# Dealing TensorE's filling work in steps of three products in a hybrid attention, SSD and gating layer

## The chip, the core and the metric

The kernel runs on one core of a Trainium2 chip. The metric is the device time of one execution in microseconds (us); lower is better. The engines are TensorE (PE in the profile, its weight loads PEld), VectorE (DVE), ScalarE (ACT), GpSimd (POOL) and SyncE (SP, which issues nearly all DMAs, strictly in the order of its row).

## What is computed

One layer for 640 tokens, 128 of a prompt and 512 of a latent grid, 2048 channels, float32. A large input projection feeds three branches; each branch's result (1024 channels) is multiplied by its own weights w_br (1024 x 2048), gated, added up and projected once more:

```python
def _layer(x, cvec, p, ctx):
    ...
    h = (_rms(x, p['g_pre']) * (1 + scale) + shift).astype(x.dtype)
    proj = jnp.matmul(h, p['w_in'])
    q, k, v, g_a, xbc, z, dt_raw, u, v_c, g_c, g_m = jnp.split(proj, _in_splits(), -1)
    ...
    o_a = o_a * jax.nn.silu(g_a)
    o_b, h_f, h_b = _ssm_branch(xbc, z, dt_raw, p, h0_f, h0_b)
    o_c = _sgu_branch(u, v_c, g_c, p)
    gate_a, gate_b, gate_c = jnp.split(jax.nn.sigmoid(g_m), 3, -1)
    merged = (gate_a * jnp.matmul(o_a, p['w_br_a']) + gate_b * jnp.matmul(o_b, p['w_br_b'])
              + gate_c * jnp.matmul(o_c, p['w_br_c']))
    y = _rms(jnp.matmul(merged, p['w_out']), p['g_post'])
    return (x + gate * y).astype(x.dtype), (k, v, h_f, h_b)
```

Branch a is attention with 16 heads (a prompt part, and a window of the grid plus 128 context keys), branch b a bidirectional state-space scan (SSD) with 16 heads and a norm over its 1024 channels, branch c a gating unit (SGU). The outputs are the layer's result, the new keys and values of the prompt and the new states of the scan.

## The kernel before

**Products.** A float32 value x is kept as two tiles, x_hi (rounded to fp32r, a ScalarE copy) and x_lo (x - x_hi, a VectorE subtraction); a product is then three fp32r products: hi by hi, hi by lo, lo by hi. Weights come in as raw tiles (wraw) and are split the same way into whi and wlo (L135 and L136). The 640 tokens are two halves of 320 columns.

**Stages.** After the projections, branch c is ready in SBUF as eight operands of 128 channels (oh, ol). The SSD (b) and the attention (a) still have to be computed. They are many small matmuls with VectorE, ScalarE and GpSimd work between, so the kernel mixes them with the long products of w_br. Those are 48 blocks: branch c, then b, then a, with 16 blocks d of 128 output channels each. A block has 8 operands k x 2 halves x 3 products = 48 products. `br_halves` (L824) is a generator that yields after each half, 24 products into one PSUM bank (tile bk); VectorE then multiplies the bank by the gate of that block (tile gt, a ring of two) and GpSimd adds it to the merged tile. `fill(n)` (L852) takes n halves from it. In the trace all these products, and those of the SSD and the attention, have the line of a helper (L807); the tile bk names the filling work, sm the rest.

**SSD** (L858 to L950). For each of the 8 pairs of heads t, `states(t)` loads tokens (xtok), lets GpSimd weight them (xw, L882), multiplies them with btok into two PSUM tiles, from which VectorE chains the states hst (L899) and ScalarE copies the new state out (so, L904); `outputs(t)` reads hst, A, E and xtok into two more PSUM tiles, VectorE makes y2, GpSimd gates it with zs, and it goes to memory as o_b. The loop runs the states one pair ahead: states(0), states(1), fill(2), outputs(0), fill(2), states(2), fill(2), outputs(1) and so on, 29 halves in all. This work's pool (ssd2) is left at its end, and the attention's pool (att) takes its place.

**Attention** (L952 to L1141). For each pair of heads j there are 5 units: b = None (prompt) and 0 to 3. A unit is `scores` (q by k, and by the context keys kc), a softmax by VectorE and ScalarE (tiles mx, s, rc; lines L990 to L997), `turned` (transposes of the probabilities, copied out as pt by ScalarE, L1081), and `values` (pt by vk and cv). Scores run one unit ahead. The list pace gives each of the 40 units a half or none, 33 in all. Pair 0's q, k, v and bias and all of kc and cv are loaded at the beginning of the attention (`loads`, L1014, and L1115, L1116), later pairs one pair ahead; the values are transposed by token (vk, L1038) by `by_tok`.

**From branch to branch.** When branch c's last block is done, branch b's operands must stand in the very slots of c's operands. `b_operands` (L958) loads the eight tiles of o_b through a staging ring of three (ost), scales each on VectorE and splits it (oh by ScalarE, L588, ol by VectorE, L589); it is called in unit 2. Its norm is a row factor that is made by `b_norm` and `b_row` and multiplied in later. Branch a's operands (oa, then oah and oal) are loaded after the last unit (L1146); two more halves of b, the rest of it, stand behind that, then a's 16 blocks, two halves each.

**Order.** The order of the matmuls is that of the text: each `step()` ties its first matmul behind the last one issued. All else is placed by a scheduler by dependences, so that a load may stand far ahead of its place in the text if its tile is free, and each engine then runs its own row in order. An engine that waits holds all that stands behind it.

## Time and profile before

| | before |
|---|---|
| runs | 2575.22, 2579.98, 2577.57 us |
| median | 2577.57 us |
| the profiled execution's own time | 2580.66 us |
| its span in the trace | 2578.9 us |
| granted TensorE clock, mean of the span | 0.987 |
| busy: PE, PEld | 95%, 89% |
| busy: DVE, ACT, POOL | 66%, 42%, 31% |
| DMA | 413.76 MB, mean 160 GB/s |

The span is what the rows of the trace cover; the device time is 1.8 us longer. A busy share is an average over the whole program. The granted clock is the share of TensorE's full speed that the chip gave it in a stretch: 1.00 is 2.4 GHz, 0.50 is 1.2 GHz. The parts that the change touches lie between 1797 and 2338 us: the SSD with c's blocks to 1955, the attention with the rest of c's blocks and nearly all of b's to 2208, then a's blocks.

### The profile page before, as it was taken

To read this page: it belongs to the slowest core of one execution; us is meant where nothing else is said; L and a number is where in the kernel's file an instruction comes from. 1 tells how busy PE (TensorE), PEld (TensorE's weight loads), DVE (VectorE), ACT (ScalarE), POOL (GpSimd) and SP (SyncE) were. 2 spreads that over 40 slices of the span, in tenths; PEclk is the share of its full clock that TensorE was granted. 3 is DMA by queue.
4 is the path that set the end of the run, shared out by engine and by line. 5 is a ranking of instruction groups with operands and counts; after the bars stand their busy time and mean duration, and the time that the engine had idled before them with its cause. 6 is when DMAs were issued, how large, how long until landed. Compare 5 with 4: busy or idle time off the path is not lost. (4 is left out here: it accounts for less than half of the span.)

```text
span 2578.9 us, 43223 instructions
## 1 busy us (share of the span) xinstructions
PE 2447.0 (95%) x16615; PEld 2306.5 (89%) x16615; DVE 1713.0 (66%) x2776; ACT 1085.4 (42%) x2343; POOL 805.5 (31%) x372
## 2 busy tenths in 40 slices
PE   6999989999999999999999999999897999999998
PEld 4579979999999999999999999989896888898886
DVE  4344678888887887777777767776334555437974
ACT  4122333444444455565555455555114555322222
POOL 2100035444444443333333434342231232331002
PEclk9999999999999999999999999999998999999999
DMA  9943533333333434534343443436777444445545
GB/s 375 340 163 106 175 119 121 103 115 114 108 108 118 142 131 145 166 132 152 126 170 122 131 155 130 143 126 210 280 254 253 165 156 124 134 125 188 190 135 167
DMA packets 152169, 413.76 MB, mean 160 GB/s; under 512 B 16981, under 2 KB 28538, under 8 KB 150938
## 3 DMA queue, kind: packets, MB, share of 16 engines
q1 hardware_dynamic: 149658, 409.95, 47.5%
q8 instruction: 130, 2.13, 0.3%
q10 hardware_dynamic: 2304, 1.05, 0.1%
q14 instruction: 77, 0.63, 0.1%
HBM read 336.12 MB, written 74.81 MB: 159 GB/s over the span
## 5 line engine op out<-in xcount | busy, mean ns | idle before, releaser
L167 DVE TENSOR_TENSOR wlo<-wraw,whi 128x512 fp32r<-128x512 f32 x448 | 613.4, 1386 | 121.8 <-ACT whi L166 113.5
L166 ACT CAST whi<-wraw 128x512 fp32r<-128x512 f32 x448 | 274.8, 616 | 313.0 <-PE acca L235 148.3
L135 ACT CAST whi<-wraw 128x512 fp32r<-128x512 f32 (+1 forms) x238 | 140.2, 592 | 412.4 <-PE bk L807 127.2
L236 PE MATMUL acca<-hh,wlo 128*128 128x320 f32 x896 | 280.8, 313 | 22.8 <-DVE wlo L167 22.7
L166 ACT CAST whi<-s 128x512 fp32r<-128x512 f32 x336 | 202.2, 617 | 199.6 <-PE sm L235 77.7
L234 PE MATMUL acca<-hh,whi 128*128 128x320 f32 x896 | 278.6, 311 | 3.9 <-ACT whi L166 3.9
L167 DVE TENSOR_TENSOR wlo<-s,whi 128x512 fp32r<-128x512 f32 x336 | 232.6, 692 | 74.6 <-ACT whi L166 70.3
L235 PE MATMUL acca<-hl,whi 128*128 128x320 f32 x896 | 277.3, 310 | 0.0
L190 POOL TENSOR_TENSOR s<-wraw 128x1024 f32<-128x1024 f32 x56 | 145.4, 2597 | 367.5 <-DMA wraw<-in_w_nt 235.7
L136 DVE TENSOR_TENSOR wlo<-wraw,whi 128x512 fp32r<-128x512 f32 (+1 forms) x218 | 147.7, 680 | 141.4 <-ACT whi L135 138.2
L191 POOL TENSOR_TENSOR s<-s,wraw 128x1024 f32<-128x1024 f32 x56 | 151.1, 2698 | 263.8 <-DVE wlo L167 263.7
L198 POOL TENSOR_TENSOR s<-wraw,s 128x1024 f32<-128x1024 f32 x56 | 138.6, 2475 | 219.0 <-issue 193.8
L236 PEld LDWEIGHTS acca<-hh,wlo 128*128 128x128 f32 x896 | 168.7, 188 | 30.4 <-DVE wlo L167 30.4
L234 PEld LDWEIGHTS acca<-hh,whi 128*128 128x128 f32 x896 | 168.8, 188 | 5.2 <-ACT whi L166 5.2
L235 PEld LDWEIGHTS acca<-hl,whi 128*128 128x128 f32 x896 | 168.8, 188 | 0.0
L807 PE MATMUL bk<-oh,whi 128*128 128x320 f32 x512 | 164.1, 321 | 0.7 <-DVE c L250 0.7
L807 PE MATMUL bk<-ol,whi 128*128 128x320 f32 x512 | 159.4, 311 | 0.0
L807 PE MATMUL bk<-oh,wlo 128*128 128x320 f32 x512 | 159.3, 311 | 0.0
L192 POOL TENSOR_TENSOR wraw<-wraw 128x1024 f32<-128x1024 f32 x56 | 152.1, 2716 | 4.3
L236 PE MATMUL sm<-t4h,wlo 128*128 128x320 f32 x448 | 141.2, 315 | 12.9 <-DVE wlo L167 12.8
L236 PE MATMUL sm<-hh,wlo 128*128 128x320 f32 x448 | 138.5, 309 | 2.8 <-DVE wlo L167 2.8
L236 PE MATMUL sm<-t12h,wlo 128*128 128x320 f32 x448 | 138.7, 310 | 1.2 <-DVE wlo L167 1.2
(390 smaller groups left out, 6978.1 us busy)
## 6 DMA issues: line engine op xcount, KB each, us to landing
wraw<-in_w_nt SPq DMA_DIRECT2D x240, 512.0 KB, 3.7
wm<-in_w_ms SPq DMA_DIRECT2D x64, 512.0 KB, 7.4
wraw<-in_w_br SPq DMA_DIRECT2D x48, 512.0 KB, 4.3
wm<-in_w_mg SPq DMA_DIRECT2D x32, 512.0 KB, 3.9
wraw<-in_w_out SPq DMA_DIRECT2D x31, 512.0 KB, 3.9
g_gate<-sg SPq DMA_DIRECT2D x48, 320.0 KB, 2.4
gt<-g_gate SPq DMA_DIRECT2D x48, 320.0 KB, 3.5
bias<-in_bias SPq DMA_DIRECT2D x8, 1152.0 KB, 7.8
```

The costliest lines, as they stand in the source:

```text
L135: S.copy(hi[:, :n], rv)
L136: eng.tensor_tensor(lo[:, :n], rv, hi[:, :n].bitcast(F32), op=ALU.subtract)
L166: S.copy(hi, src[:, i:i + 512])
L167: V.tensor_sub(lo, src[:, i:i + 512], hi.bitcast(F32))
L190: G.tensor_tensor(s1, a21, a22, op=ALU.add)
L191: G.tensor_tensor(s2, s1, a11, op=ALU.subtract)
L192: G.tensor_tensor(a21, a11, a21, op=ALU.subtract)
L198: G.tensor_tensor(s2, a12, s2, op=ALU.subtract)
L234: TE.matmul(ps, wh, bh, start=(k == 0 and i not in (2, 3)), stop=False, skip_group_check=True)
L235: TE.matmul(ps, wh, bl, start=False, stop=False, skip_group_check=True)
L236: mm = TE.matmul(ps, wl, bh, start=False, stop=(k == n - 1), skip_group_check=True)
L807: newest[0] = TE.matmul(*args, **kw)
```

## The change

The unit of filling becomes a step: the three products of one operand and one half (`br_steps` in place of `br_halves`), and all counts are given in steps, eight to a half.

- **SSD.** `weighted` (xtok and xw) is cut off from `states`. The order is now fill(16), then for each pair states(t), weighted(t+1), fill(8), outputs(t), fill(24); after outputs(6) it is fill(8), after outputs(7) none. That is 232 steps, as many products as the 29 halves.
- **First attention tiles.** In pair 6's place of the text `first_loads(0)` loads kc for pair 0 alone (64 KB; kc now comes by pairs) and the first of three rows of the bias (b0) into the outer pool, and q, k, v of pair 0 into two free slots and one tile of ost. The other two rows of the bias are loaded with `loads`.
- **Attention.** fill(8) stands before the first scores; the pace is 8, 8 and then 6 or 7 steps in each of the other 38 units, 248 steps. The 24 steps that are left of branch b stand behind the last unit, fill(24).
- **Passage by the contraction.** In blocks 0 and 15 of each branch the operand k is the outer loop and the half the inner one, with a PSUM bank for each half, so that operand k is read in two neighbouring steps. In all other blocks the halves come one after the other, as before.
- **b's operands** are asked for in unit 1; ScalarE scales while it rounds (one activation) and VectorE subtracts with the scaling in one instruction, so eight VectorE multiplications are dropped. The staging ring ost has two tiles instead of three. b_norm and b_row are each called a unit or two earlier.
- **Buffers.** Gates (gt) 2 to 3; xtok 2 to 3; xT, btok, xw 2 to 1; the operands oa of branch a pass through a ring of four instead of eight tiles. The four columns of a softmax stand in one tile.

```diff
     def gate_ring(name):
-        return p2.tile([P, T], F32, tag="gt", name=name, bufs=2)
+        return p2.tile([P, T], F32, tag="gt", name=name, bufs=3)
+    def ost(name):
+        return p2.tile([P, T], F32, tag="ost", name=name, bufs=2)
...
-        for s in range(2):
+        ps = [None, None]
+        ks = [(k, s) for k in range(8) for s in range(2)] if d in (0, KD - 1) else [(k, s) for s in range(2) for k in range(8)]
+        for k, s in ks:
             hs = (H1, H2)[s]
+            if k == 0:
+                ps[s] = bank()[:, :HALF]
+            (wh, wl), (oh, ol) = ws[k], branch["abc"[b]][k]
             with step():
...
+                for w, x, first, last in ((wh, oh, k == 0, False), (wh, ol, False, False), (wl, oh, False, k == 7)):
+                    mm(ps[s], w, x[:, hs], start=first, stop=last)
...
+    def first_loads(j):
+        x = {}
+        x["kc"] = p2.tile([P, P], F32, tag="kc", name="kc", bufs=2)
+        nc.sync.dma_start(out=x["kc"], in_=a["cache_k"][:, j, :])
+        x["b0"] = p2.tile([P, 2, 384], F32, tag="b0", name="b0", bufs=2)
+        nc.sync.dma_start(out=x["b0"], in_=a["bias"][:, 2 * j:2 * j + 2, 0, :])
+        return x
...
-            r = s2.tile(list(shape), F32, tag=tag, name=tag)
+            r = s2.tile(list(shape), F32, tag=tag, name=tag, bufs={"btok": 1, "xT": 1, "xtok": 3}.get(tag, 2))
...
+        def weighted(t):
+            x_tok = load("xtok", xk_dram[:, t, :])
+            xw = [s2.tile([P, T], F32, tag=f"xw{d}", name=f"xw{d}", bufs=1) for d in range(2)]
...
-        fill(2)
-        st_t = states(0)
+        xs = weighted(0)
+        fill(16)
         for t in range(8):
-            nxt = states(t + 1) if t < 7 else None
-            fill(2 if t < 7 else 1)
+            st_t = states(t, *xs)
+            if t < 7:
+                xs = weighted(t + 1)
+            if t == 6:
+                J[0] = first_loads(0)
+                J[0]["qT"] = kqv(slot(14, F32, "qT0"), 16)
+                J[0]["kT"] = kqv(slot(15, F32, "kT0"), 0)
+                J[0]["vT"] = kqv(ost("vT0"), 8)
+            fill(8)
             outputs(t, *st_t)
-            fill(2 if t < 6 else 0)
-            st_t = nxt
+            fill((24, 8, 0)[max(t - 5, 0)])
...
-                t = p2.tile([P, T], F32, tag="ost", name="ost", bufs=3)
+                t = ost("ob")
...
-                V.tensor_scalar_mul(t, t, g_)
-                split_to((hi, lo), t)
+                S.activation(hi, t, AF.Copy, scale=g_)
+                V.scalar_tensor_tensor(out=lo, in0=t, scalar=g_, in1=hi.bitcast(F32), op0=ALU.mult, op1=ALU.subtract)
...
-        pace = [1] * 3 + [0] * 2 + [0 if i % 7 == 3 else 1 for i in range(35)]
+        pace = [8, 8] + [232 * (i + 1) // 38 - 232 * i // 38 for i in range(38)]
+        fill(8)
         scores(0, None)
...
-            if i == 2:
+            if i == 1:
                 b_operands()
...
-        t = pa.tile([P, T], F32, name=f"oa{k}")
+        t = pa.tile([P, T], F32, tag="oa", name="oa", bufs=4)
...
-    fill(2)
+    fill(24)
...
-        fill(2)
+        fill(16)
```

ScalarE's row at the beginning of the SSD, before. The lines L904 copy new states out of the PSUM tiles of one `states` (two for each pair); L135 splits weights, L936 squares y.

```order
L904 COPY so<-sm_19206 128x128
L905 DMA out_new_state_fwd<-so 128x128
L904 COPY so<-sm_19222 128x128
L905 DMA out_new_state_bwd<-so 128x128
L135 CAST whi<-wraw 128x512 x2
L904 COPY so<-sm_19254 128x128
L904 COPY so<-sm_19270 128x128
L905 DMA out_new_state_fwd<-so 128x128
L905 DMA out_new_state_bwd<-so 128x128
L936 ACTIVATE zs<-y_19387 128x640
```

The same place in the changed kernel:

```order
L930 COPY so<-sm_19206 128x128
L931 DMA out_new_state_fwd<-so 128x128
L930 COPY so<-sm_19222 128x128
L931 DMA out_new_state_bwd<-so 128x128
L135 CAST whi<-wraw 128x512
L962 ACTIVATE zs<-y_19319 128x640
L135 CAST whi<-wraw 128x512 x3
L930 COPY so<-sm_19421 128x128
```

The second pair of copies stood before the first pair's y; it stands behind it now, with three weight splits between.

SyncE's row at the beginning of the attention, before: the first q, k, v, bias, kc and cv stand behind the next to last o_b of the SSD.

```order
L935 DMA o_b<-y_20683 128x640
L933 DMA zs<-sl_b 128x640
L1001 DMA qT<-kqv_d 128x640
L1001 DMA kT<-kqv_d 128x640
L1001 DMA vT<-kqv_d 128x640
L1017 DMA bias<-in_bias 128x2304
L935 DMA o_b<-y_20759 128x640
L1115 DMA kc<-in_cache_k 128x1024
L1116 DMA cv<-in_cache_v 128x1024
```

In the changed kernel four of these stand far ahead, among the first SSD loads of the row (A, E, xtok), or ahead of those:

```order
L866 DMA kT_20554<-kqv_d 128x640
...
L886 DMA E_19457<-mx_d 128x640
L886 DMA xtok<-xk_d 128x640
L125 DMA wraw<-in_w_br 128x1024 x2
L872 DMA kc<-in_cache_k 128x128
L874 DMA b_20550<-in_bias 128x2x384
L866 DMA vT_20556<-kqv_d 128x640
L830 DMA gt<-g_gate 128x640
```

Only the bias rows 1 and 2 and cv still stand where the SSD ends.

ScalarE's row at the passage from c to b, before. The eight oh are b's operands; s and pt belong to the softmax and the transposes of the units.

```order
L994 ACTIVATE s,sum<-s,nm 128x384
L588 CAST oh_21067<-ost 128x640
L997 ACTIVATE s<-s,rc 128x384
L588 CAST oh_21074<-ost 128x640
L588 CAST oh_21081<-ost 128x640
L135 CAST whi<-wraw 128x512
L997 ACTIVATE s<-s,rc 128x384
L135 CAST whi<-wraw 128x512
L1081 COPY pt<-sm_21161 128x384
L1081 COPY pt<-sm_21166 128x384
L588 CAST oh_21088<-ost 128x640
```

And now (L997 is the activation that scales and rounds, L1105 the copy pt):

```order
L997 ACTIVATE oh_21005<-ob,pc 128x640
L1025 ACTIVATE s<-s,mx 128x384
L135 CAST whi<-wraw 128x512
L997 ACTIVATE oh_21011<-ob,pc 128x640
L1105 COPY pt<-sm_20967 128x384
L1105 COPY pt<-sm_20972 128x384
L1023 ACTIVATE s,mx<-s,mx 128x384 x2
L1025 ACTIVATE s<-s,mx 128x384 x2
L997 ACTIVATE oh_21017<-ob,pc 128x640
L135 CAST whi<-wraw 128x512
L997 ACTIVATE oh_21023<-ob,pc 128x640
L997 ACTIVATE oh_21029<-ob,pc 128x640
```

Three operands in a row stood ahead of two pt before, with an s between the first two; now two stand ahead of the first two pt, and three more ahead of the next two.

## Rows read from the trace of the kernel before

**Rows 1.** The page, part 1: busy us (share of span) xinstructions, by engine.

```profile
PE 2447.0 (95%) x16615; PEld 2306.5 (89%) x16615; DVE 1713.0 (66%) x2776; ACT 1085.4 (42%) x2343; POOL 805.5 (31%) x372
```

**Rows 2.** Windows by stage: from:to, us, PE PEld DVE ACT POOL, clock, DMA, GB/s.

```profile
1797.40:1955.50 158.10, 145.98 (x1240) 140.79 (x1240) 61.69 (x172) 27.64 (x54) 46.67 (x30) 0.98 0.77 264
1955.50:1971.30 15.80, 8.01 (x33) 6.14 (x34) 4.43 (x19) 5.01 (x15) 3.06 (x2) 0.57 0.91 332
1971.30:2005.40 34.10, 28.37 (x205) 23.65 (x204) 21.19 (x58) 21.10 (x49) 2.97 (x2) 0.85 0.62 229
2005.40:2207.90 202.50, 194.31 (x1554) 171.57 (x1554) 101.93 (x358) 117.88 (x308) 58.56 (x35) 0.99 0.44 139
2207.90:2230.70 22.80, 16.36 (x87) 14.97 (x88) 10.43 (x16) 7.08 (x11) 7.94 (x5) 0.78 0.64 220
```

**Rows 3.** Windows of the four longest stretches at the lower clock, same columns.

```profile
1810.82:1817.63 6.81, 2.99 (x13) 3.02 (x14) 1.16 (x7) 0.27 (x1) 0.00 (x0) 0.50 1.04 404
1957.59:1971.23 13.64, 7.94 (x32) 6.07 (x33) 3.68 (x18) 4.94 (x15) 2.85 (x2) 0.50 0.99 364
1995.14:2005.36 10.22, 7.54 (x35) 5.74 (x36) 6.93 (x18) 6.19 (x16) 1.79 (x1) 0.50 0.68 272
2220.42:2230.64 10.22, 5.23 (x18) 4.88 (x19) 1.38 (x4) 1.35 (x2) 3.06 (x2) 0.50 0.33 110
```

**Rows 4.** Waits of PE, 1797 to 2231 us: releaser: total us, times, longest.

```profile
PE sm L807 <- ACT so L904: 7.1, 2, 4.7
PE sm L810 <- ACT s L997: 5.7, 3, 3.7
PE sm L807 <- POOL xw L882: 5.0, 8, 0.7
PE bk L807 <- ACT oah L588: 4.9, 1, 4.9
PE sm L807 <- ACT pt L1081: 4.6, 8, 1.1
```

**Rows 5.** Timeline of PE, products of one half: start us, us, instruction.

```profile
1944.73 0.31 PE L807 MATMUL bk<-oh,whi 128*128 128x320 f32 x1
...
1945.17 0.31 PE L807 MATMUL bk<-oh,whi 128*128 128x320 f32 x1
```

**Rows 6.** Timeline of PE: the first products of the outputs of three pairs.

```profile
1824.13 0.66 PE L807 MATMUL sm<-E,xtok 128*64 128x128 f32 x8
...
1843.21 0.66 PE L807 MATMUL sm<-E,xtok 128*64 128x128 f32 x8
...
1864.04 0.66 PE L807 MATMUL sm<-E,xtok 128*64 128x128 f32 x8
```

**Rows 7.** Timeline of DVE: the chain of states of one pair.

```profile
1835.58 2.38 DVE L899 SCALAR_TENSOR_TENSOR hst<-hst,cdec,sm 128x64 f32<-128x64 f32 x12
```

**Rows 8.** Waits of POOL, 1840 to 1930 us.

```profile
POOL xw L882 <- DMA xtok<-xk_d: 14.8, 4, 3.9
```

**Rows 9.** One load of ost (1994 us), and timelines of ACT and DVE there.

```profile
DMA to landing us min/median/max: 6.2/6.2/6.2
...
1993.32 0.72 ACT L588 CAST oh<-ost 128x640 fp32r<-128x640 f32 x1
...
1994.12 0.82 DVE L589 TENSOR_TENSOR ol<-ost,oh 128x640 fp32r<-128x640 f32 x1
```

**Rows 10.** The load of qT at 1956 us.

```profile
DMA to landing us min/median/max: 2.9/2.9/2.9
```

**Rows 11.** Timelines of PE and ACT in one unit: its scores, its last scaling.

```profile
2050.42 0.71 PE L807 MATMUL sm<-kT,qT 64*128 64x256 f32 x4
...
2055.13 0.62 ACT L997 ACTIVATE s<-s,rc 128x384 f32<-128x384 f32 x1
```

**Rows 12.** Timelines of SP and ACT: the last operand of branch a.

```profile
2218.62 0.39 SPq L1148 DMA_DIRECT2D oa<-o_a  x1
...
2224.41 0.72 ACT L588 CAST oah<-oa 128x640 fp32r<-128x640 f32 x1 [6.12 <-DMA oa<-o_a]
```

More of the change, by code (lines that the diff above doesn't have):

```diff
@@ L844, in br_halves, with all_steps, kqv @@
             yield
-    def all_halves():
+    def all_steps():
         for b in (2, 1, 0):
             for d in range(KD):
-                yield from br_halves(b, d)
-    halves_left = all_halves()
+                yield from br_steps(b, d)
+    steps_left = all_steps()
     def fill(n):
         for _ in range(n):
-            next(halves_left)
+            next(steps_left)
+    def kqv(t, i):
+        nc.sync.dma_start(out=t, in_=kqv_dram[:, i, :])
+        return t
+    def first_loads(j):
[5 more added lines that the diff above has]
+        return x
@@ L858, in hybrid_step @@
+    J = {}
     with ExitStack() as ph:
@@ L876, in states @@
             b_tok = btok[0]
-            hs = slice(2 * t, 2 * t + 2)
-            x_tok = load("xtok", xk_dram[:, t, :])
-            xw = [s2.tile([P, T], F32, tag=f"xw{d}", name=f"xw{d}") for d in range(2)]
-            for d in range(2):
-                G.tensor_tensor(by_head(xw[d]), by_head(x_tok),
-                                wst[:, d, :, hs].unsqueeze(3).to_broadcast([P, NCH, 2, 64]), op=ALU.mult)
             hst = []
@@ L955, in hybrid_step @@
         cv = a1.tile([P, 1024], F32, name="cv")
-        kc = a1.tile([P, 8, P], F32, name="kc")
         def b_operands():
@@ L987, in b_row, with softmax @@
             nc.sync.dma_start(out=ssq, in_=rstd_d.rearrange("c p -> (c p)").unsqueeze(0).to_broadcast([P, T]))
-        def softmax(s, mx):
-            nm = at.tile([P, 1], F32, tag="nm", name="nm", bufs=4)
-            V.tensor_scalar_mul(nm, mx, -1.0)
-            sm = at.tile([P, 1], F32, tag="sum", name="sum", bufs=4)
-            S.activation(s, s, AF.Exp, bias=nm, accum_out=sm)
-            rc = at.tile([P, 1], F32, tag="rc", name="rc", bufs=4)
-            V.reciprocal(rc, sm)
-            S.activation(s, s, AF.Copy, scale=rc)
-        def kqv(i, tag):
-            t = at.tile([P, T], F32, tag=tag, name=tag)
-            nc.sync.dma_start(out=t, in_=kqv_dram[:, i, :])
-            return t
+        def softmax(s, v):
+            V.tensor_scalar_mul(v[:, 1:2], v[:, 0:1], -1.0)
+            S.activation(s, s, AF.Exp, bias=v[:, 1:2], accum_out=v[:, 2:3])
+            V.reciprocal(v[:, 3:4], v[:, 2:3])
+            S.activation(s, s, AF.Copy, scale=v[:, 3:4])
         def loc(t, col, n):
@@ L1009, in es_ @@
             return slice(64 * e, 64 * e + 64)
-        J = {}
         def loads(j):
-            J[j] = {"qT": kqv(16 + j, "qT"), "kT": kqv(j, "kT"), "vT": kqv(8 + j, "vT")}
-            bj = at.tile([P, 2, 3, 384], F32, tag="bias", name="bias")
-            nc.sync.dma_start(out=bj, in_=a["bias"][:, 2 * j:2 * j + 2])
+            if j:
+                J[j] = first_loads(j)
+                for n, i in (("qT", 16 + j), ("kT", j), ("vT", 8 + j)):
+                    J[j][n] = kqv(at.tile([P, T], F32, tag=n, name=n), i)
+            bj = at.tile([P, 2, 2, 384], F32, tag="bias", name="bias")
+            nc.sync.dma_start(out=bj, in_=a["bias"][:, 2 * j:2 * j + 2, 1:3, :])
             J[j]["bias"] = bj
```

43 lines of the change are left out of this document (22 added, 21 removed).

## The prediction

> **What bounds the kernel now.** TensorE does: its products fill 2447.0 of 2578.9 us, 95% [rows 1]. So I looked for the places where it is not filled, cut the program there into stages, and read each stage's time, busy time and granted clock [rows 2]. Up to 1797.4 us and after 2230.7 the change leaves the order of the work as it was. Between the two, the five stages lose, as time minus TensorE's busy time, 12.1 us (SSD), 7.8 (first attention units), 5.7 (from branch c to b), 8.2 (rest of the attention) and 6.4 (from b to a): 40.3 us idle.
>
> The clock takes more. It falls to its lower level (1.2 instead of 2.4 GHz) in stretches that begin in or just after long waits, and the four longest [rows 3] have a granted clock of 0.50 throughout. Work done there would have taken half as long, so half of the busy time is lost: 2.99/2 = 1.5 us in the SSD, 7.94/2 = 4.0 at the start of attention, 7.54/2 = 3.8 from c to b, 5.23/2 = 2.6 from b to a; 11.9 us. A gap thus costs more than its length. Idle and slow time together, 52 us, is all that a new order can give back, since the same products are run before and after; the list of waits [rows 4] tells what each gap waited for.
>
> **What the change does, part by part.** A product of 320 columns follows the last one after (1945.17 - 1944.73)/3 = 0.147 us [rows 5]; a step of three is 0.44 us, a half of 24 products 3.52 us, a block of 48 7.04 us. Their number stays 2304.
>
> *SSD.* Before, the states of pair 0 and pair 1 stood back to back, and the second set needs the PSUM tiles that ScalarE's copies so must empty: 7.1 us in two waits [rows 4], and 1.5 us of slow clock behind them. Now 32 steps and the outputs lie between, some 17 us, and this goes: 8.6 us. From pair 3 on TensorE also waited for GpSimd's weighted inputs xw, eight waits, 5.0 us [rows 4]. What that costs whole is read from the distance of two outputs: 1843.21 - 1824.13 = 19.08 us without such a wait, 1864.04 - 1843.21 = 20.83 with it [rows 6]; 1.75 x 4 pairs = 7.0 us. Now xw of the next pair is issued before the fill of 8 and the outputs and 24 more steps, 14 us + 3, against 3.5 us of GpSimd work, so it goes too. Together 15.6 us.
>
> What is late next: the states are now followed by only 8 steps, 3.5 us, before the outputs read hst. Its twelve VectorE operations take 2.38 us [rows 7] and stand behind one evacuation (about 0.5 us), one cast and one wlo (about 0.6 and 0.7 us): done some 4.0 us after the block's end, while TensorE asks for them at 2.0 (states) + 3.5 + 0.3 = 5.8 us. The cover is 1.8 us, so I cost the edit at nothing; without the cover it would be paid eight times. Single buffers of xT, xw and btok also cost nothing: xT of the next pair is asked for when y of this one is done and has most of 19 us.
>
> Against this term speaks a rule of the Trainium skill, Perfetto Trace Analysis, Optimization Strategy: a gap that repeats for a stretch on the engine that should be full can mean too few buffers for the next tile. By it the xw gap would stay, since this change takes buffers away, and the sum would be 7.0 us smaller. The trace does not agree: the engine behind the gap, GpSimd, itself waited for xtok from memory, 14.8 us in four waits, the longest 3.9 [rows 8], and xtok is the one tile that gets a third buffer.
>
> *Start of attention.* Its tiles lay in the pool that the SSD had just left, so no load could start before the last output; 7.8 us idle and 4.0 slow. Now q, k, v, the context keys and the first bias of pair 0 come from other places while the SSD runs: about 1.4 MB more (worked out from the tile shapes) in a stretch at 264 GB/s where the next stage ran at 332 [rows 2], so they fit. Eight steps (3.5 us) stand between the last outputs and the first scores and cover y, which must free a PSUM tile. The other bias rows and cv are still asked for late, but are first read some 11 and 16 us after the last outputs. A wait for the copy of vk and one for the first softmax stay, about 1.3 us. Gain 11.8 - 1.3 = 10.5 us.
>
> *From c to b.* Before: 5.7 idle + 3.8 slow = 9.5 us. Now operand k of c is free after its own two steps, and b asks for one every two steps, six steps a unit. That removes the rule that all eight must be ready, but the eight tiles of o_b now pass through two staging buffers instead of three, and v of pair 0 occupies one of them until it is transposed. A round of two is load, ScalarE 0.72, VectorE 0.82 [rows 9], then the next load. With a load of 2.9 us, as in an empty queue [rows 10], a round is 4.6 us and three units of some 5.3 us cover it nearly; with 6.2 us, as here [rows 9], it is 7.9 us and TensorE starves. Worse, ScalarE's row has oh of operands 2, 3 and 4 ahead of the pt copies for unit 1's values: a late load holds up the softmax as well. I placed ScalarE's operations one after another for both lengths and get 5 us of stalls with the short load and 11 with the long one, plus 2 to 4 us of slow clock: 7 to 15 us against 9.5. I take 9.5, no gain, since the rows nearest to it are the long ones at its first half and the queue empties later; the bounds are +3 and -6.
>
> *Rest of attention.* Before, 8.2 idle and about 1.5 slow (half of the slow 1% x 2 of 202.5 us, less its own idle time). Most of the waits are for pt in units without fill (pt 4.6 us over all [rows 4]). Now each unit has 6 or 7 steps, 2.64 us or more, in place of 3.52 or none. That is enough if the softmax is: from the start of a unit's scores to its last scaling 2055.13 + 0.62 - 2050.42 = 5.3 us [rows 11], against 0.9 + 0.6 + 2.64 + 0.8 + 0.9 + 0.3 = 6.1 us of products until it is read (own scores, the transposes, fill, values, next scores, first head's transposes, each read beside these rows). The cover is 0.8 us. The waits of 0.25 us for vk stay, some 2.7 us in all. Gain 7 us.
>
> *From b to a.* The last tile of o_a was loaded behind a weight load that waited for its buffer; its load went out at 2218.62 and ScalarE split it at 2224.41 [rows 12], the wait of 4.9 us [rows 4]. Now 24 steps (10.6 us) follow the last values instead of two halves (7.0 us), and the first block of a asks for operand 7 at its step 15, 6.2 us in, instead of 3.1. That is 6.6 us more cover, above the 4.9 that were missing, and it takes the two waits for earlier operands with it. Gain 6.4 + 2.6 - 0.5 = 8.5 us.
>
> *Third gate buffer, scalings and softmax columns.* The first lets gates be loaded a block earlier; no row shows TensorE waiting for one, so nothing. Eight VectorE multiplications fewer, half a microsecond each, and fewer small tiles lie beside TensorE's work: nothing. The last block of a now ends both halves together, but its result is the sixteenth operand of w_out, asked for far later: nothing.
>
> **The sum.** 15.6 + 10.5 + 0 + 7 + 8.5 = 41.6 us. The profiled execution took 2580.66 us (span 2578.9), 3.1 above the median of the three runs, 2577.57. So 2539 on its own scale, 2536 on the median's; I say 2538.
>
> **The rivals.**
> - *The passage starves.* 15 us lost from c to b, and a second slow stretch behind it: 6 to 11 us more than in the sum, 2547. For it speaks the load of 6.2 us, against it that the queue is emptier then.
> - *The repeating gap stays,* because the order or the buffers leave GpSimd late again, as by the page's rule: 2538 + 7 = 2545. Against it rows 8.
> - *Six steps are too short a cover.* If ScalarE's casts push the softmax 0.5 us past its cover of 0.8, each of 32 units with a window waits that long: 16 us, 2554. ScalarE is busy 117.9 of 202.5 us there [rows 2], which speaks against it.
> - *Early loads don't come early.* If SP, which issues in order, holds the first attention tiles behind a gate or weight load, the start keeps its 10.5 us: 2548.
> - *Slower than before: hst is late at every output.* If VectorE stands before hst at an evacuation whose gate has not landed, all eight outputs wait. With W the delay, TensorE loses 8 x (W - 1.8). It decides from W = 7.0 us: 8 x 5.2 = 41.6. At 8 us: 8 x 6.2 = 50 us, 2587. The third gate buffer speaks against it: a gate is asked for some 12 us before it is read.
>
> **How the numbers follow.** My forecast (2528 to 2546) has 0.62, the starved passage 0.15, the staying gap 0.06, the short cover 0.07, the late loads 0.06, the late hst 0.04. If every gap closed, the time would be 2580.66 - 52 - 3 = 2525; with rivals added to one another up to 2555: the range is 2525 to 2555. Faster or slower by 0.2%, 5 us, is about what a measurement of this kernel can tell from no change. All cases but the last are faster by more; for stacked mishaps I leave some: faster 0.93, same 0.03, slower 0.04.
>
> **What would show it.** Right: no wait for so or xw in the SSD, outputs 19.1 us apart, its stage some 142 us; the first scores within 4 us of the last outputs at full clock; in the passage, waits for ol, pt or s of 5 to 11 us with staging loads just before them; no units with over 0.5 us of waiting after it; no wait for oah. Wrong: waits for hst in the outputs, waits for s in every unit, or a slow stretch that starts where no wait stood before.

## The result and the profile after

The changed kernel takes 2534.55 us (median; 2531.71 to 2537.36) against 2577.69 before: 43.1 us less, ratio 0.9833 with the 95% interval 0.9816 to 0.985. The forecast was 2538, range 2525 to 2555. The profiled execution took 2532.52 us, span 2530.7. Its page, part 1, answers to [rows 1]:

```profile
PE 2433.7 (96%) x16615; PEld 2301.3 (91%) x16615; DVE 1718.7 (68%) x2768; ACT 1085.7 (43%) x2343; POOL 804.6 (32%) x372
```

To see where the time went I cut both programs at the same work. TensorE's filling products can be counted in its timeline, and the attention's units stand at known places among them, so five cuts can be set: branch c's first product, the end of the last outputs, the beginning of unit 1's filling, product 1465 of all (the 1537th is a's first) and product 1633, the 97th of branch a. Windows between the cuts, before (the SSD, 158.08 us from cut to cut, is the first of [rows 2]), columns as in [rows 2]:

```profile
1955.46:1975.39 19.93, 12.10 (x65) 9.71 (x66) 6.87 (x26) 6.80 (x19) 3.06 (x2) 0.66 0.93 345
1975.39:2203.27 227.88, 213.97 (x1690) 187.38 (x1688) 119.17 (x408) 135.14 (x350) 61.26 (x36) 0.97 0.46 151
2203.27:2239.07 35.80, 29.36 (x184) 27.60 (x182) 15.60 (x23) 11.11 (x18) 10.28 (x6) 0.86 0.49 164
```

and of the changed kernel, SSD first:

```profile
1792.45:1934.30 141.85, 141.85 (x1241) 138.94 (x1241) 64.98 (x169) 27.45 (x54) 42.92 (x30) 1.00 0.87 303
1934.30:1949.36 15.06, 13.33 (x100) 11.86 (x100) 8.46 (x28) 7.93 (x20) 4.27 (x3) 1.00 0.87 324
1949.36:2160.31 210.95, 204.03 (x1667) 179.80 (x1666) 117.03 (x400) 134.61 (x349) 61.13 (x36) 0.98 0.51 165
2160.31:2189.60 29.29, 26.54 (x170) 26.28 (x169) 18.01 (x23) 10.39 (x16) 11.44 (x6) 0.94 0.65 213
```

Three pieces of work lie on the other side of a cut in the changed kernel, and are put back before the stretches are compared. 24 more filling products (3.52 us) and the ten products of `b_norm` (ssq, 1.21 us) stand ahead of unit 1's filling. The values of the last unit (0.89 us) stand ahead of product 1465; before, they stood behind it.

| stretch | predicted gain | measured gain |
|---|---|---|
| SSD | 15.6 | 158.08 - 141.85 = 16.2 |
| start of attention | 10.5 | 19.93 - (15.06 - 3.52 - 1.21) = 9.6 |
| c to b and rest of attention | 0 + 7 | (227.88 - 3.52 - 1.21 + 0.89) - 210.95 = 13.1 |
| b to a | 8.5 | (35.80 - 0.89) - 29.29 = 5.6 |
| sum | 41.6 | 44.5 |

The third row can be parted at the values of unit 5. From the values of unit 1 to there TensorE took 22.0 us before, 1.2 of them b_norm's, and 18.4 now, its filling products left out at 0.147 us each: the passage gained 2.4. From there to the values of the last unit it took 96.8 and 86.0: the rest of the attention gained 10.8. Of these, 6.4 are idle time (8.2 before, 1.7 now).

The two profiled spans differ by 48.2 us, 3.7 more than the stretches. These 3.7 are not the change's: 4.9 of them lie ahead of the first cut, and -1.3 behind the last. Branch c's first product came at 1797.38 and 1792.45 us, and in the fourteen profiled executions of this study, whose products up to there are the same, it came anywhere between 1786.55 and 1797.68. That scatter is why the experiments below are judged by the stretches first.

The stretches scatter less, but not by nothing. The last 672 products of branch a took 98.41 or 98.42 us in all fourteen executions. The start of the attention, however, took 16.5 and 16.6 us in two of the runs below, with the same order of products there as in the changed kernel (15.06 us) and the same one wait in it: the clock fell once, as here in the run with eight steps or none.

```profile
1939.96:1943.37 3.41, 3.41 (x18) 3.12 (x15) 1.41 (x7) 2.23 (x8) 0.00 (x0) 0.50 1.04 418
```

Such a stretch costs 1.7 us, so a difference below that between two single executions is not called an effect.

TensorE's waits after the SSD, in the same form as [rows 4], are now these:

```profile
PE sm L810 <- DVE rrow L1016: 4.8, 1, 4.8
PE bk L807 <- DVE gt L846: 2.8, 1, 2.8
PE sm L810 <- ACT vk L1061: 1.9, 7, 0.3
PE sm L810 <- DVE mx L1022: 1.7, 1, 1.7
PE sm L810 <- DVE vk L1061: 0.2, 1, 0.2
```

The clock's two stretches at the lower level there, as in [rows 3]:

```profile
1957.22:1964.05 6.83, 4.96 (x22) 4.36 (x23) 4.79 (x12) 4.04 (x9) 0.00 (x0) 0.50 0.69 235
2175.68:2179.09 3.41, 3.41 (x15) 3.41 (x14) 3.07 (x2) 1.01 (x3) 3.03 (x2) 0.50 0.60 220
```

In the SSD there is no wait: 141.85 us, all of it busy, clock 1.00. The waits for so, xw, s, pt and oah are gone. Of the single waits that are left, mx is the only one at the start, where the first softmax and the copy of vk were expected to leave 1.3 us. Two are new, each with a stretch at the lower clock in or behind it: rrow (the row factor of branch b, at 1954 us, in the passage from c to b) and gt (the emptying of a PSUM bank, at 2171 us, at a's first block).

### The profile page after: what moved, and what is told of

It is laid out like the page before. It is cut to its first block, busy times and chain, and to the rows that moved or that the text cites. A ratio compares the mean times of both kernels' runs of the same rounds, so it can differ in the third digit from the quotient of the medians.

```text
span 2530.7 us, 43237 instructions
## 1 busy us (share of the span) xinstructions
PE 2433.7 (96%) x16615; PEld 2301.3 (91%) x16615; DVE 1718.7 (68%) x2768; ACT 1085.7 (43%) x2343; POOL 804.6 (32%) x372
## 4 chain that ended last, share of the span: by engine, by line
PE 72%; DVE 9%; DMA 8%; issue 5%; ACT 3%; SPq 0%; POOL 0%; POOLq 0%; DVEq 0%; ACTq 0%
PE bk L807 12%; PE sm L236 5%; PE sm L234 5%; PE sm L235 5%; PE acca L236 5%; PE acca L234 4%; PE acca L235 4%; PE accb L236 4%; DVE wlo L167 4%; PE accb L234 4%; PE accb L235 4%; PE sm L807 3%; PE sm L1266 2%; PE sm L1267 2%; PE sm L1265 2%
## 5 line engine op out<-in xcount | busy, mean ns | idle before, releaser
L135 ACT CAST whi<-wraw 128x512 fp32r<-128x512 f32 (+1 forms) x238 | 140.1, 592 | 421.2 <-PE bk L807 142.1
L136 DVE TENSOR_TENSOR wlo<-wraw,whi 128x512 fp32r<-128x512 f32 (+1 forms) x218 | 156.8, 722 | 148.5 <-ACT whi L135 147.8
```

The lines of the kernel that those rows point to most:

```text
L135: S.copy(hi[:, :n], rv)
L136: eng.tensor_tensor(lo[:, :n], rv, hi[:, :n].bitcast(F32), op=ALU.subtract)
```

## The experiments

"Start", "middle" and "end" are the three stretches behind the SSD: 15.06, 210.95 and 29.29 us in the changed kernel, 255.3 together.

### The SSD: order or buffers

**The new order alone, in the kernel before.** `weighted` is split off as in the change, with all buffers as before:

```diff
-        fill(2)
-        st_t = states(0)
+        xs = weighted(0)
+        fill(2)
         for t in range(8):
-            nxt = states(t + 1) if t < 7 else None
-            fill(2 if t < 7 else 1)
+            st_t = states(t, *xs)
+            if t < 7:
+                xs = weighted(t + 1)
+            fill(1)
             outputs(t, *st_t)
-            fill(2 if t < 6 else 0)
-            st_t = nxt
+            fill((3, 1, 0)[max(t - 5, 0)])
```

> The kernel before with the SSD's new order alone, in halves as before: states(t), weighted(t+1), fill(1), outputs(t), fill(3); xtok keeps two tiles, xw two each. Theory 'order': what made TensorE wait for so and for xw was that states stood one pair ahead, so both waits go: outputs 19.05 to 19.1 us apart throughout, the SSD stage 142 us in place of 158.1, 16 us faster than before (some 2562). Rival 'buffers': the wait for so goes (8.6 us, 2569), but xw stays late from pair 3 on, outputs 20.8 us apart, because xtok has no third tile.

Median 2559.72 us, ratio to before 0.9937 (0.9912 to 0.9961). The SSD took 141.8 us. Outputs of neighbouring pairs in TensorE's timeline, where [rows 6] had 20.83 us between the last two:

```profile
1847.56 0.66 PE L807 MATMUL sm<-E,xtok 128*64 128x128 f32 x8
...
1866.60 0.66 PE L807 MATMUL sm<-E,xtok 128*64 128x128 f32 x8
```

19.04 us, as between all pairs up to the last, with no wait but the first product's own. The order alone gives all that the SSD gained, 16.3 us, with two tiles of xtok. It leaves little to spare, though: VectorE, which must finish hst before the outputs read it, waited six times for a gate in the SSD here, twice in the changed kernel with its third gate tile (second line):

```profile
DVE m L839 <- DMA gt<-g_gate: 11.6, 6, 2.8
DVE m L846 <- DMA gt<-g_gate: 3.3, 2, 2.0
```

At its tightest output hst was ready 0.25 us ahead of its first reader in this run (a scaling of ost stood between, too). The third gate tile was not tried alone.

**A third tile for xtok alone, in the kernel before.**

```diff
-            r = s2.tile(list(shape), F32, tag=tag, name=tag)
+            r = s2.tile(list(shape), F32, tag=tag, name=tag, bufs=3 if tag == "xtok" else 2)
```

> The kernel before with a third tile for xtok and nothing else. Theory 'late load': GpSimd was late because xtok could only be loaded once the outputs of the pair before had read its tile; a third tile then takes away the eight waits for xw, 7 us, some 2570, and the wait for so stays. Rival 'order': GpSimd's own work stands too late in the program; xw waits stay, 2577. If both this and the new order alone cure xw, either would have been enough.

Median 2571.94 us, ratio 0.9986 (0.9972 to 1.0). SSD 152.34 us, 5.7 less. TensorE's waits of the SSD:

```profile
PE sm L807 <- ACT so L904: 7.6, 2, 4.6
PE bk L807 <- DVE c L250: 1.9, 1, 1.9
```

xw is gone and so is left. So either would have cured xw, and only the order cures so. The outputs came 19.04 us apart throughout, in place of 20.83 four times: 7.3 us for xw. The stage gained less, since its first outputs came 1.6 us later than before, behind the waits for so and a longer slow stretch there. The rule that the prediction weighed (the Trainium skill, Perfetto Trace Analysis, Optimization Strategy: a repeating gap can mean too few buffers) names one of the two cures rightly; it doesn't follow that the gap must stay where no buffer is added, as the run before shows.

### The start: early tiles or covering steps

Before, TensorE waited at the start for these two:

```profile
PE sm L807 <- ACT zs L936: 4.9, 1, 4.9
PE sm L807 <- DMA kc<-in_cache_k: 2.2, 1, 2.2
```

The first of them, 1955.5 to 1960.3 us, ended with two things at once: ScalarE's zs was done at 1959.7, and the first keys, asked for at 1956.65, landed 3.4 us later, at 1960.0.

**q, k and v of pair 0 late again.** The three `kqv` lines of pair 6 are dropped, and `loads(0)` loads these tiles into the attention's pool:

```diff
                 J[0] = first_loads(0)
-                J[0]["qT"] = kqv(slot(14, F32, "qT0"), 16)
-                J[0]["kT"] = kqv(slot(15, F32, "kT0"), 0)
-                J[0]["vT"] = kqv(ost("vT0"), 8)
```

> The changed kernel, but q, k and v of pair 0 lie in the attention's pool again, as before, so that they are loaded after the SSD has left its own; kc and the first bias row still come early, and ost is free for b's operands from the start. Theory: the first scores wait 6 to 9 us for their loads beyond the 8 steps that now cover some of it, and the clock falls behind the wait: 6 to 10.5 us slower than the changed kernel (2541 to 2545). Rival: the 8 steps alone cover the loads, under 2 us slower; or b's operands gain from the free ost tile what the start loses.

Median 2530.09 us, ratio 0.9823 (0.9801 to 0.9846). Start 15.79 us, only 0.7 more; all three stretches 256.6, 1.3 more. The theory fell: taken alone, the early tiles are worth no more than the scatter.

**The eight steps behind the first scores.**

```diff
-        pace = [8, 8] + [232 * (i + 1) // 38 - 232 * i // 38 for i in range(38)]
-        fill(8)
+        pace = [16, 8] + [232 * (i + 1) // 38 - 232 * i // 38 for i in range(38)]
         scores(0, None)
```

> The changed kernel with the 8 steps ahead of the first scores moved behind them, into unit 0, which then has sixteen; pair 0's tiles still come early. Theory 'cover': the steps, not the early loads, cured the start, because the first scores need PSUM tiles that the last outputs' y must empty and the keys' tile the pool that the SSD leaves: 2 to 5 us slower than the changed kernel. Rival 'early tiles': with q, k and v there already the steps hide nothing: under 1.5 us.

Median 2536.71 us, ratio 0.9846 (0.9821 to 0.9871). Start 16.85 us, 1.8 more; all three 258.4, 3.1 more. That is within what was expected of the cover, but little above the scatter.

**Both undone together**, by the two edits above.

> The changed kernel with both cures of the start undone together: q, k and v of pair 0 in the attention's pool again, and the 8 steps moved behind the first scores. kc and the first bias row still come early. From the last output to the 97th product of branch a the changed kernel takes 255.3 us; with late q, k, v alone it took 256.6, with the steps moved alone 258.4. Theory 'either suffices': each covers what the other would, so that the loss of both together is 8 to 12 us, 263 to 267 us in that stretch, with 6 us or more of waiting for the loads at the start and a slow stretch behind it. Rival 'additive': 4 to 5 us, about 260; then most of the gain at the start is owed to neither, but to kc and the bias being cut into pieces.

Median 2536.9 us, ratio 0.9845 (0.982 to 0.9869). Two of TensorE's waits, and the window of the slow stretch (as in [rows 3]):

```profile
PE sm L807 <- DMA kT<-kqv_d: 4.9, 1, 4.9
...
PE sm L810 <- DMA vT<-kqv_d: 2.1, 1, 2.1
```

```profile
1941.17:1951.41 10.24, 6.98 (x29) 5.38 (x30) 3.44 (x17) 3.42 (x12) 0.33 (x1) 0.50 0.96 346
```

Start 24.06 us: 9.0 more, where the two alone add up to 2.5. Either covers for the other, as the theory had it, in the start. The kernel before, with the 3.52 and 1.21 us of work that have moved there, would stand at 24.66: the two covers are nearly all of the gain, and the smaller first pieces of kc and the bias, which stay early in this run, at most 0.6. But the middle is 3.3 us shorter (207.62), because branch b's operands are loaded while TensorE waits at the start: the third oh began 0.1 us before the middle, in the changed kernel 7.7 us into it, and rrow's wait is 2.0 instead of 4.8 us. All three stretches together lose 5.9 us, not the 8 to 12 that I had expected.

### Even filling

**Eight steps or none in each unit.**

```diff
-        pace = [8, 8] + [232 * (i + 1) // 38 - 232 * i // 38 for i in range(38)]
+        pace = [8, 8] + [8 * (29 * (i + 1) // 38 - 29 * i // 38) for i in range(38)]
```

> The changed kernel with its attention units filled by eight steps or none, as before, in place of 6 or 7 each: 29 of the last 38 units have eight, nine have none; all else as changed. Theory: units without filling make TensorE wait for pt or s, 0.5 to 1 us in each of nine, with a slow stretch now and then: 5 to 8 us slower than the changed kernel (2540 to 2543). Rival: the waits in the rest of the attention came from elsewhere (vk, late loads), and eight or none is no worse: under 2 us.

Median 2544.01 us, ratio 0.9872 (0.9849 to 0.9895). The middle took 222.19 us, 11.2 more, all three stretches 12.2 more, of which some 1.5 are the slow stretch at the start shown above. Waits that the changed kernel doesn't have:

```profile
PE sm L807 <- ACT pt L1105: 7.4, 11, 1.1
...
PE sm L810 <- ACT s L1025: 2.2, 3, 1.0
```

The cause was right and the size half of what it is: an empty unit costs more than one short wait. From one unit's values to the next, less the filling, each of the eight empty units from unit 6 on and the unit behind it took 1.4 to 1.9 us longer together than in the changed kernel. The rest of the attention, from the values of unit 5 on, took 98.5 us, with the kernel before at 96.8: the even filling is the whole gain there.

### The passage from c to b

The row that ends in rrow's wait, in the changed kernel: TensorE's transpose of rcol and the next thing it does, ScalarE's oh of the third operand, and VectorE's row.

```profile
1954.02 0.27 PE L810 MATMUL sm<-cm,rcol 128*5 128x128 f32 x1
1959.09 0.47 PE L810 MATMUL sm<-cm,kT 128*128 128x128 f32 x1 [4.80 <-DVE rrow L1016]
```

```profile
1957.10 0.83 ACT L997 ACTIVATE oh<-ob,pc 128x640 fp32r<-128x640 f32 x1 [1.29 <-DMA ob<-o_b]
```

```profile
1957.96 0.88 DVE L998 SCALAR_TENSOR_TENSOR ol<-ob,pc,oh 128x640 fp32r<-128x640 f32 x1 [2.18 <-ACT oh L997]
1958.76 0.27 DVE L1016 COPY rrow<-sm 5x128 f32<-5x128 f32 x1
```

rrow's copy, 0.27 us, was ready to go at 1954.3. It stood in VectorE's row behind ol, ol behind oh, oh behind a load; and TensorE's transpose of the next keys needs the one PSUM tile that the copy empties. Four runs asked what the price hangs on.

**The half as the outer loop in all blocks.**

```diff
-        ks = [(k, s) for k in range(8) for s in range(2)] if d in (0, KD - 1) else [(k, s) for s in range(2) for k in range(8)]
+        ks = [(k, s) for s in range(2) for k in range(8)]
```

> The changed kernel with the half as the outer loop in all blocks, 0 and 15 too. Theory: at the passage from c to b all eight operands must stand ready within the first 24 products, and operand k of c is free only 8 steps later than now, so TensorE waits for ol or oh of b's operands 5 to 10 us more, at a lower clock behind it: 5 to 15 us slower (2540 to 2550). From b to a: operand 7 is asked for 3 us earlier, 1 to 3 us more of waiting. Rival: the loads of o_b, not the freeing of the slots, set the passage, so that the wait only moves: under 3 us.

Median 2540.25 us, ratio 0.9862 (0.9839 to 0.9884). Middle 3.1 us longer, end 2.2 longer. TensorE's longest wait is now for oh:

```profile
PE bk L807 <- ACT oh L997: 4.8, 2, 4.5
```

So the contraction as the outer loop is worth 5.3 us in this pair of executions, two fifths of it at b to a, where the slow stretch was 6.83 us long in place of 3.41.

**b_row after unit 3.**

```diff
-            if i == 1:
+            if i == 3:
                 b_row(rcol)
```

> The changed kernel with the row factor's transpose (b_row) put after unit 3 in place of unit 1. Theory 'one bad place': the wait of 4.8 us for rrow and the slow stretch behind it (2.5 us) come from VectorE's copy of rrow, which stands behind ol of a late operand; moved out of the passage, both go, 5 to 7 us faster (2528 to 2530). Rival 'late operands': the loads of o_b set the pace, so TensorE waits a little later for ol or oh of operands 3 to 5 instead, and less than 3 us are won.

Median 2530.34 us, ratio 0.9821 (0.9798 to 0.9843). rrow's wait is gone, and the three stretches took 255.8 us, 0.5 more. The start is 1.5 longer by the slow stretch named above, ahead of the edit; the middle is 0.8 shorter. There the time now lies in a wait for oh and a longer one for vk, with two stretches of 3.41 us at the lower clock in place of one of 6.83.

```profile
PE sm L810 <- ACT vk L1061: 3.4, 7, 1.8
...
PE sm L810 <- ACT oh L997: 1.9, 1, 1.9
```

The rival, late operands, was right: less than 3 us were won.

**One tile for the bias rows 1 and 2**, so that pair 1's come after the passage.

```diff
-            bj = at.tile([P, 2, 2, 384], F32, tag="bias", name="bias")
+            bj = at.tile([P, 2, 2, 384], F32, tag="bias", name="bias", bufs=1)
```

> The changed kernel with one tile in place of two for the rows 1 and 2 of the bias, so that pair 1's 786 KB are loaded only after pair 0's last scores and no longer just ahead of b's operands. Theory 'late operands': the loads of o_b land 2 to 4 us earlier without that transfer beside them, and the wait for rrow shrinks from 4.8 to 1 to 3 us with its slow stretch: 2 to 6 us faster than the changed kernel. Rival: the ring of two staging tiles sets their pace, not the transfer beside them: within 1.5 us; or the bias is then late at the next pair's scores, 1 to 3 us for each of seven pairs.

Median 2531.86 us, ratio 0.9817 (0.9788 to 0.9845). rrow's wait shrank to 0.6, but TensorE waited 2.7 us for rcol and 2.1 for a vk: start 3.1 longer, middle 1.7 shorter, 1.3 more in all. The SSD took 143.17 us, with one wait of 0.9 us for hst in it; the account of the SSD below comes back to that.

**Three staging tiles, two of xtok.**

```diff
-        return p2.tile([P, T], F32, tag="ost", name=name, bufs=2)
+        return p2.tile([P, T], F32, tag="ost", name=name, bufs=3)
...
-            r = s2.tile(list(shape), F32, tag=tag, name=tag, bufs={"btok": 1, "xT": 1, "xtok": 3}.get(tag, 2))
+            r = s2.tile(list(shape), F32, tag=tag, name=tag, bufs={"btok": 1, "xT": 1, "xtok": 2}.get(tag, 2))
```

> The changed kernel with three staging tiles (ost) for b's operands, as before the change, the room taken from xtok, which has two tiles again. SSD: by the run with the new order alone xtok's third tile is not needed there, so the SSD stays at 141.9 us; if it is needed, xw waits come back, up to 7 us. Passage, theory 'ring': with two tiles a load can only start when the one before last has been split; with three the operands are ready 3 to 7 us earlier, the wait of 4.8 us for rrow shrinks to under 2.5, and the stretch from the last output to the 97th product of a is 2 to 6 us shorter than 255.3. Rival 'queue': the loads land as late whatever tile they have, since they share the DMA engines with the rest: within 1.5 us.

Median 2530.54 us, ratio 0.9831 (0.9811 to 0.9851). The SSD stayed at 141.86: the third xtok tile was not needed. The last oh began at 1964.7 instead of 1969.8 us, yet the slowest load took as long to land (7.5 us, 7.3 in the changed kernel), rrow's wait is 4.5 us and the three stretches took 255.4. So none of the three single cures won anything alone: two moved the wait to another link, the third hardly shortened it.

### From b to a

**Operands of a early, the last one in place.**

```diff
-                nc.sync.dma_start(out=o_dram["a"][:, j, :], in_=oT)
+                if j < 7:
+                    nc.sync.dma_start(out=o_dram["a"][:, j, :], in_=oT)
...
-        t = pa.tile([P, T], F32, tag="oa", name="oa", bufs=4)
-        nc.sync.dma_start(out=t, in_=o_dram["a"][:, k, :])
+        if k < 7:
+            t = slot(14, F32, "oa0") if k == 0 else ost("oa") if k < 3 else pa.tile([P, T], F32, tag="oa", name="oa", bufs=4)
+            nc.sync.dma_start(out=t, in_=o_dram["a"][:, k, :])
+        else:
+            t = J[7]["oT"]
```

> The changed kernel with branch a's first three operands loaded into tiles that are free during the attention (a slot and the two staging tiles), the next four through the ring of four at once, and the last one split from the tile in SBUF without the way through memory; the same values. Theory: TensorE's wait of 2.8 us for the evacuation of a bank stands behind oal of operands whose loads waited for the ring; so it goes with its slow stretch: from a's first to its 97th product 14 to 15.5 us in place of 18.6, some 4 us faster. Rival: the evacuation is late because of VectorE's own load there (weights' splits and eight oal), and under 1.5 us is won.

Median 2532.94 us, ratio 0.9838 (0.9821 to 0.9854). a's first 96 products took 16.81 us in place of 18.62. The slow stretch behind the wait did not come, which is 1.7 of these 1.8 us, and whether the edit kept it away is open. The wait for gt stayed, 2.5 us: the loads were not its cause.

### All together

```diff
-        ks = [(k, s) for k in range(8) for s in range(2)] if d in (0, KD - 1) else [(k, s) for s in range(2) for k in range(8)]
+        ks = [(k, s) for k in range(8) for s in range(2)] if d == 0 or (d == KD - 1 and b == 2) else [(k, s) for s in range(2) for k in range(8)]
...
-        fill(8)
+        fill(4)
+        by_tok(0, 0)
+        by_tok(0, 1)
+        fill(4)
         scores(0, None)
-        for part in range(3):
-            by_tok(0, part)
+        by_tok(0, 2)
```

with b_row after unit 3, one bias tile, three staging tiles and two of xtok, and a's operands early. The transposes of pair 0's keys and values (`by_tok`) ahead of the first scores, and block 15 of b and a with the halves one after the other, are new here and were not run alone.

> The changed kernel with what the runs so far point to, together: three staging tiles (xtok two), the bias rows 1 and 2 in one tile, b_row after unit 3, the transposes of pair 0's keys and first values between the 8 steps ahead of the first scores, branch a's operands loaded early as in the run before and the last one split in place, and the contraction as the outer loop in block 15 of branch c alone, not of b and a. Theory for the passage: the single cures only moved the wait along one row of loads and splits; together they shorten it, 3 to 6 us less from the last output to b's block 15. Theory for b to a: the wait of 2.5 to 2.8 us for a bank comes from three banks for two blocks that each hold two: block 15 of b gives both back only at its end, while VectorE is at the operands' splits; with the halves one after the other there it goes, and a's first 96 products take 14.1 to 15.5 us in place of 16.8 (18.6 in the changed kernel). In all 245 to 250 us from the last output to a's 97th product in place of 255.3, and 5 to 10 us faster than the changed kernel, about 2527. Rivals: the passage's waits move again (under 2 us there, 250 to 252); VectorE's splits, not the banks, hold a's first block (16.5 us or more).

Median 2522.29 us (2514.07 to 2528.33), ratio to before 0.9793 (0.9776 to 0.981): faster than the changed kernel too, whose interval to before lies above. Windows of start, middle and end, and all of TensorE's waits in them:

```profile
1938.84:1954.27 15.43, 13.72 (x99) 12.21 (x100) 9.95 (x31) 9.50 (x23) 3.73 (x3) 1.00 0.88 322
1954.27:2157.71 203.44, 201.41 (x1668) 177.70 (x1666) 114.16 (x398) 133.12 (x347) 61.15 (x36) 1.00 0.53 173
2157.71:2186.22 28.51, 26.55 (x171) 26.29 (x169) 18.77 (x23) 10.09 (x16) 11.29 (x6) 0.94 0.53 169
```

```profile
PE bk L807 <- DVE gt L846: 2.0, 1, 2.0
PE sm L810 <- ACT vk L1061: 1.8, 7, 0.3
PE sm L810 <- ACT s L1025: 1.7, 2, 1.0
PE sm L810 <- DVE vk L1061: 0.2, 1, 0.2
```

247.4 us in all, 7.9 less. In the middle the cures that gave -0.8, -1.7 and -0.4 us one by one give 7.5 with the others, at full clock throughout, and all of it between the values of units 1 and 5. That fits a passage that is one chain of loads, splits and copies, of which several links had to be shortened at once. Which of them could be left out again was not tried, nor what the earlier transposes have in it.

At a's first block the theory of the banks fell. VectorE's row there:

```profile
2163.68 0.48 DVE L846 SCALAR_TENSOR_TENSOR gt<-gt,bk 128x320 f32<-128x320 f32 x1
2164.08 0.82 DVE L589 TENSOR_TENSOR oal<-oT,oah 128x640 fp32r<-128x640 f32 x1
2164.82 2.20 DVE L589 TENSOR_TENSOR oal<-oa,oah 128x640 fp32r<-128x640 f32 x1
2166.94 2.07 DVE L136 TENSOR_TENSOR wlo<-wraw,whi 128x512 fp32r<-128x512 f32 x1
2168.94 1.55 DVE L589 TENSOR_TENSOR oal<-oa,oah 128x640 fp32r<-128x640 f32 x2
2170.41 0.47 DVE L846 SCALAR_TENSOR_TENSOR gt<-gt,bk 128x320 f32<-128x320 f32 x1
```

The first bank of b's block 15 had its last product at 2164.7 us and was emptied at 2170.41: VectorE was at it without a pause, but at the splits of a's operands, which stood ahead in its row. TensorE waited 2.0 us (its first 96 products of a: 17.85 us), as the rival said. What is left to move there is the place of the splits in VectorE's row; that was not tried.

## Why the prediction was right, step by step

**SSD, 15.6: right, 16.2.** Both waits went, and the order did it. The reason that I gave for xw (xtok's third tile) would do alone, 7.3 us by the distance of the outputs for 7.0 foreseen, but wasn't needed. The cover of 1.8 us for hst held at seven of the eight outputs, 1.7 to 2.2 us. At pair 1's it was only 0.55, from the end of VectorE's twelve operations to TensorE's first reading:

```profile
1821.56 2.38 DVE L925 SCALAR_TENSOR_TENSOR hst<-hst,cdec,sm 128x64 f32<-128x64 f32 x12
```

```profile
1824.49 0.61 PE L807 MATMUL sm<-A,hst 128*64 128x128 f32 x8
```

VectorE was late because ScalarE's casts were. ScalarE had stood between its two copies so, by the profile until the first bias tile, one of the early loads, had landed:

```profile
1814.72 0.27 ACT L930 COPY so<-sm 128x128 f32<-128x128 f32 x1 [9.55 <-DMA b<-in_bias]
```

In the run with one bias tile ScalarE stood there for 10.26 us, and TensorE waited 0.9 us for hst. So the early tiles may not have come free, which I had not priced; no run loads the bias tile late to show it. The mechanism of the rival on the slower side, a gate that VectorE waits for ahead of hst, showed in the run of the order alone: with two gate tiles the cover was 0.25 to 0.92 us at five outputs. The third gate buffer, put at nothing, cost and won no time that a run shows, but seems to be what keeps the cover.

**Start, 10.5: right, 9.6; its cause only half right.** I put it on the early loads and let the eight steps cover y. The runs show two covers of which either is nearly enough: 0.7 and 1.8 us alone, 9.0 for both.

**Passage and rest of attention, 0 + 7: mis-sized, 2.4 + 10.8.** The even filling is the larger term: the run with eight or none lost 11.2 us in this stretch. I had counted TensorE's idle time (8.2) and half the slow time (1.5), less 2.7 us of waits that would stay. The idle time left is 1.7, and half the slow time was 1.7. The other 2.7 us of the 10.8 lie in what the profile calls busy; no run parts them further. The passage did starve as bounded: 4.8 us for rrow and half of the 4.96 us of slow work in and behind it, 7.3 us, within my 7 to 15 and 2.2 below the 9.5 of before. But it starved at a place that I had not priced at all: the change calls b_row two units earlier, and its copy waits in VectorE's row behind the operands' splits. The mechanism that I described for ScalarE and pt worked one engine further on.

**b to a, 8.5: mis-sized, 5.6.** The wait for oah went, but a new one for a bank came, 2.8 us with 1.7 of slow time behind it. I followed the loads, and not VectorE's row, where the emptying of the banks stands behind splits of a's operands. That the 24 steps behind the last unit took the wait for oah away is argued from the cover; they were not undone alone.

**The sum.** The terms were off by +0.6 (SSD), -0.9 (start), +2.4 (passage), +3.8 (rest) and -2.9 us (b to a); the time missed the forecast by 3.5 us because they partly cancelled, not because each was known that well. The rivals "short cover" (no wait for s is left) and "late loads" (they came early, and late ones alone cost 1.3 us, not 10.5) didn't happen; "the passage starves" happened in part.

## What to carry to other kernels

A gap on the bottleneck engine can have two cures, each enough alone or nearly so, as xw's and the start's had here: undo them one by one and neither seems to matter, undo both and the gap is back. When filling work can be cut finer, spread it evenly: a unit without filling cost more here than its one named wait, in part in the unit behind it. And where a change brings operands in at a seam, read the in-order row of every engine that prepares them: the victim is the short, unrelated instruction behind them, here a copy of 0.27 us and the emptying of a bank.

## What the runs showed of the hardware

A split on VectorE that begins while GpSimd is at work can take up to three times as long. In the row above, oal took 0.82 us once and 2.20 the next time, and wlo 2.07; where it came first the same wlo took 0.68:

```profile
2170.80 0.68 DVE L136 TENSOR_TENSOR wlo<-wraw,whi 128x512 fp32r<-128x512 f32 x1
```

GpSimd's row at that time:

```profile
2164.24 2.10 POOL L849 TENSOR_TENSOR gt<-gt,ssq 128x640 f32<-128x640 f32 x1 [4.05 <-DVE gt L846]
2166.41 2.05 POOL L850 TENSOR_TENSOR m<-m,gt 128x640 f32<-128x640 f32 x1
```

The slow oal ends at 2167.02, 0.68 us after GpSimd's gt (2166.34), and the slow wlo at 2169.01, 0.55 after m (2168.46). That is as if each had begun its work only when GpSimd was done, and it is so throughout: in the last kernel's stretches seventeen wlo began behind a running GpSimd instruction, took 0.89 to 2.07 us, and all ended 0.55 us after it. Nine began up to 0.2 us ahead of GpSimd's gt or m; they took 0.68 or 0.69 us, and it was GpSimd that took longer, 1.93 to 2.08 us against 1.54 at the least, as in its first row here, beside the oal of 0.82. So the one that comes first runs undisturbed. The Trainium skill says so (SBUF — State Buffer, Who interferes with whom: a VectorE instruction with two inputs in SBUF contends with a GpSimd instruction that reads SBUF, what they share is an exclusive lock, and the order of issue decides who blocks), and these rows agree. The 2.8 us that the two splits lost there (2.20 + 2.07 - 0.82 - 0.68) are more than the wait of 2.0 us for the bank.

The clock: a wait did not always bring a slow stretch. Behind the same wait of 1.73 us at the start it stayed at 1.00 in the changed kernel and fell to 0.50 for 3.41 us in two other runs. After 2.8 us for gt in the changed kernel 3.41 us ran at the lower level, after 2.0 us in the last kernel as much, after 2.5 us in the run with a's operands early none. In the SSD without waits it stayed at 1.00 for 141.85 us.
